# Adaptive average pooling: the sum over a tile in one VectorE instruction in place of a sum shared with GpSimd

## The chip, the cores and the metric

The kernel runs on one core of one Trainium2 chip. The metric is device time in microseconds (us), the median over several runs. One further execution was taken by the hardware profiler; durations below come from that one execution.

## The reference

The input `x` is float32, 32 x 256 x 4096. Each row of 4096 is cut into 256 windows of 16 neighbours, and each window is replaced by its mean:

```python
for i in range(output_size):                       # 256
    start = int(i * length / output_size)          # 16 * i
    end = int((i + 1) * length / output_size)
    result[:, :, i] = np.mean(x[:, :, start:end], axis=-1)
```

134.2 MB are read and 8.4 MB written. There is one addition per element read, and one multiplication per window.

## The kernel before

The 32 x 256 = 8192 rows are spread over 128 partitions. A tile is `xin`, 128 partitions by 16384 numbers (4 rows of 4096 each), or 1024 windows ("cells") of 16 in each partition, 8.39 MB. There are 16 tiles, in one Python loop over `t` that is written out in full. The pool `inpool` has two buffers for `xin`, so tile t+2 goes into the buffer of tile t.

Each turn of the loop issues, in this order:

- L74: the load of the tile, on SyncE's queue. It waits until its buffer's last reader is done.
- in the last turn only (t = 15), behind the load, the store `o_many` of the results of tiles 0 to 13 (`res_many`, 7.34 MB), by the helper at L61. It waits for ScalarE's scaling of tile 13.
- L77: GpSimd folds the upper half of the cells: in cells 512 to 1023, it adds the last 8 numbers of each window to the first 8, in place.
- L82: VectorE sums windows of 16 in the lower half of the cells (8192 numbers per partition).
- L85: VectorE sums the folded windows of 8 in the upper half (4096 numbers per partition). It waits for L77.
- L88: ScalarE multiplies the tile's 1024 sums by 1/16, in place in `res`.

After the loop the store `o_few` sends the results of tiles 14 and 15 (`res_few`, 1.05 MB), again by L61. All loads and stores are issued by SyncE in program order. The order of the rest follows from each engine's program order and from the semaphores that the tile framework puts in. The last reader of a tile is L85, and so L85 is what lets SyncE issue the load two tiles on.

Of the kernel before, what the change touches and what calls it, by code (L numbers as in the profile page):

```python
# [1 line left out]

# [4 lines left out]


@with_exitstack
def kernel(  # L10
    ctx: ExitStack,
    tc: tile.TileContext,
    x: bass.AP,
    output_size: int,
    out: bass.AP,
):

    nc = tc.nc
    F32 = mybir.dt.float32
    X = mybir.AxisListType.X

    batch, channels, length = x.shape
    ob, oc, olen = out.shape
    assert ob == batch and oc == channels and olen == output_size
    assert length % output_size == 0
    window = length // output_size  # L30
    hw = window // 2
    inv_w = 1.0 / float(window)

    P = nc.NUM_PARTITIONS
    R = 4
    tail = 2
    rows = batch * channels
    assert rows % (P * R) == 0
    ntiles = rows // (P * R)
    head = ntiles - tail  # L40
    many = head * R
    few = tail * R
    cells = R * output_size
    m = cells // 2
    cols = R * length

    xr = x.rearrange("b c l -> (b c) l")
    orow = out.rearrange("b c o -> (b c) o")
    x_many = xr[0 : P * many, :].rearrange("(p r) l -> p (r l)", p=P, r=many)
    o_many = orow[0 : P * many, :].rearrange("(p r) o -> p (r o)", p=P, r=many)  # L50
    x_few = xr[P * many :, :].rearrange("(p r) l -> p (r l)", p=P, r=few)
    o_few = orow[P * many :, :].rearrange("(p r) o -> p (r o)", p=P, r=few)

    res_many = nc.alloc_sbuf_tensor("res_many", [P, head * cells], F32, align_bytes=256)
    res_few = nc.alloc_sbuf_tensor("res_few", [P, tail * cells], F32, align_bytes=256)
    inpool = ctx.enter_context(tc.tile_pool(name="inpool", bufs=2))

    stored = nc.alloc_semaphore("stored")

    def store(out, in_):  # L60
        ins = nc.sync.dma_start(out=out, in_=in_)  # L61
        tc.no_tile_sem_insts.add(ins.ins.name)
        ins.then_inc(stored, 16)

    for t in range(ntiles):
        k = t - head
        xin = inpool.tile([P, cells, window], F32, name="xin")
        if k < 0:
            res, base = res_many, t * cells
            src = x_many[:, t * cols : (t + 1) * cols]  # L70
        else:
            res, base = res_few, k * cells
            src = x_few[:, k * cols : (k + 1) * cols]
        nc.sync.dma_start(out=xin.rearrange("p o w -> p (o w)"), in_=src)  # L74
        if t == ntiles - 1:
            store(o_many, res_many[:, :])
        nc.gpsimd.tensor_add(  # L77
            out=xin[:, m:cells, 0:hw],
            in0=xin[:, m:cells, 0:hw],
            in1=xin[:, m:cells, hw:window],  # L80
        )
        nc.vector.reduce_sum(  # L82
            out=res[:, base : base + m], in_=xin[:, 0:m, :], axis=X
        )
        nc.vector.reduce_sum(  # L85
            out=res[:, base + m : base + cells], in_=xin[:, m:cells, 0:hw], axis=X
        )
        nc.scalar.mul(  # L88
            out=res[:, base : base + cells],
            in_=res[:, base : base + cells],  # L90
            mul=inv_w,
        )
    store(o_few, res_few[:, :])

    ctx.pop_all().close()
    tc.close()
    tc.compile()  # L97
    nc.sync.wait_ge(stored, 32)
    nc.sync.sem_clear(stored)


# [1 line left out]
_INS = ['x', 'output_size']  # L103
_OUTS = [((32, 256, 256), 'float32')]

_NUMBERS = {'output_size': 256}


# [26 lines left out]
```

## Time and profile before

| | |
|---|---|
| median of 3 runs | 333.56 us (333.36 to 333.82) |
| time of the profiled execution | 333.14 us |
| its span in the profile | 331.8 us |
| moved by DMA | 142.61 MB, a mean of 430 GB/s |
| DMA engines' time in packets | 99.4% of 16 engines' span |
| VectorE busy | 209.7 us, 32 instructions |
| GpSimd busy | 139.7 us, 20 instructions, 16 of them the fold |
| ScalarE busy | 18.2 us |

The span is the stretch that the profile covers; the profiled execution took 1.3 us more than its span, and 0.4 us less than the median. Engine names in the profile: DVE is VectorE, POOL is GpSimd, ACT is ScalarE, SP is SyncE, and SPq is SyncE's sequencer as it issues DMAs. L82 is line 82 of the kernel. A group's line gives the tile written and the tile read with their shapes, the number of instructions, their busy time in us and the mean of one in ns, and then the engine's idle time just before them with what ended it.

### The profile page before, as it was taken

How to read it: one execution, taken by the hardware profiler on the slowest of the kernel's cores; microseconds unless marked ns; L12 is line 12 of the kernel's file. 1: busy time of each engine (PE TensorE's matmuls, PEld its weight loads, DVE VectorE, ACT ScalarE, POOL GpSimd, SP SyncE). 2: the span in 40 equal slices, each digit the busy share in tenths (PEclk: the TensorE clock that was granted, in tenths of full speed). 3: DMA queues.
4: the chain of work that ended last, by engine and by line, in shares of the span. 5: the costliest groups of instructions: out<-in, count | busy, mean ns of one | idle time of the engine just before them, and what ended most of it. 6: DMA issues, size and time to landing. Idle time of an engine off the chain costs nothing.

```text
span 331.8 us, 159 instructions
## 1 busy us (share of the span) xinstructions
DVE 209.7 (63%) x32; ACT 18.2 (5%) x17; POOL 139.7 (42%) x20
## 2 busy tenths in 40 slices
DVE  0029396692939669392966939295693929569392
ACT  1000101001010100001010000101000010100001
POOL 0027090642709164270906437090643709063370
DMA  9898989989898998989899898989899898989998
GB/s 379 379 506 379 506 379 411 474 379 506 379 506 379 427 458 379 506 379 506 379 458 427 379 506 379 506 379 498 387 403 482 379 506 379 506 379 442 411 442 348
DMA packets 2592, 142.61 MB, mean 430 GB/s; under 512 B 288, under 2 KB 288, under 8 KB 288
## 3 DMA queue, kind: packets, MB, share of 16 engines
q1 hardware_dynamic: 2592, 142.61, 99.4%
HBM read 134.22 MB, written 8.39 MB: 430 GB/s over the span
## 4 chain that ended last, share of the span: by engine, by line
DMA 66%; POOL 18%; DVE 11%; POOLq 3%; issue 0%; ACT 0%; SPq 0%
DMA xin<-in_x_dram 66%; POOL xin L77 18%; DVE res_many L85 9%; POOLq L97 3%; DVE res_few L85 1%; ACT res_few L88 0%; SPq L74 0%; POOLq L77 0%
## 5 line engine op out<-in xcount | busy, mean ns | idle before, releaser
L77 POOL TENSOR_TENSOR xin<-xin 128x4096 f32<-128x4096 f32 x16 | 139.5, 8717 | 181.4 <-DMA xin<-in_x_dram 181.4
L82 DVE TENSOR_REDUCE res_many<-xin 128x512 f32<-128x8192 f32 x14 | 121.6, 8686 | 101.3 <-DMA xin<-in_x_dram 101.3
L85 DVE TENSOR_REDUCE res_many<-xin 128x512 f32<-128x4096 f32 x14 | 61.9, 4420 | 2.3 <-POOL xin L77 2.1
L88 ACT ACTIVATE res_many<-res_many 128x1024 f32<-128x1024 f32 x14 | 14.8, 1056 | 271.3 <-DVE res_many L85 271.3
L82 DVE TENSOR_REDUCE res_few<-xin 128x512 f32<-128x8192 f32 x2 | 17.4, 8686 | 12.1 <-DMA xin<-in_x_dram 12.1
L85 DVE TENSOR_REDUCE res_few<-xin 128x512 f32<-128x4096 f32 x2 | 8.8, 4420 | 0.3 <-POOL xin L77 0.3
L88 ACT ACTIVATE res_few<-res_few 128x1024 f32<-128x1024 f32 x2 | 2.1, 1056 | 36.6 <-DVE res_few L85 36.6
L88 ACT ACT_TABLE_LOAD x1 | 1.3, 1283 | 0.7 <-PEq L116 0.7
L116 POOL MEMSET const-float32-0.0<- 128x1 f32 x1 | 0.1, 98 | 0.2 <-issue 0.2
L116 POOL MEMSET const-uint8-127<- 128x1 uint8 x1 | 0.1, 102 | 0.0
L116 POOL MEMSET const-bfloat16-1.0<- 128x1 bf16 x1 | 0.1, 101 | 0.0
L116 POOL MEMSET const-float32-1.0<- 128x1 f32 x1 | 0.1, 99 | 0.0
## 6 DMA issues: line engine op xcount, KB each, us to landing
out_dram<-res_many SPq DMA_DIRECT2D x1, 7168.0 KB, 41.2
out_dram<-res_few SPq DMA_DIRECT2D x1, 1024.0 KB, 4.9
xin<-in_x_dram SPq DMA_DIRECT2D x16, 25.4
```

Of the source, the lines that this page charges most:

```text
L77: nc.gpsimd.tensor_add(out=xin[:, m:cells, 0:hw], in0=xin[:, m:cells, 0:hw], in1=xin[:, m:cells, hw:window],)
L82: nc.vector.reduce_sum(out=res[:, base : base + m], in_=xin[:, 0:m, :], axis=X)
L85: nc.vector.reduce_sum(out=res[:, base + m : base + cells], in_=xin[:, m:cells, 0:hw], axis=X)
L88: nc.scalar.mul(out=res[:, base : base + cells], in_=res[:, base : base + cells], mul=inv_w,)
L97: tc.compile()
L116: nc = _bacc.Bacc("TRN2", target_bir_lowering=False, num_devices=1)
```

## The change

GpSimd's fold (L77) and the second sum (L85) are taken out. VectorE sums all 1024 windows of 16 in one instruction (16384 numbers per partition). The loads, the stores, the scaling, the two buffers and the order of the loop stay as they are.

```diff
-    hw = window // 2
...
-    m = cells // 2
...
         nc.sync.dma_start(out=xin.rearrange("p o w -> p (o w)"), in_=src)
         if t == ntiles - 1:
             store(o_many, res_many[:, :])
-        nc.gpsimd.tensor_add(
-            out=xin[:, m:cells, 0:hw],
-            in0=xin[:, m:cells, 0:hw],
-            in1=xin[:, m:cells, hw:window],
-        )
-        nc.vector.reduce_sum(
-            out=res[:, base : base + m], in_=xin[:, 0:m, :], axis=X
-        )
-        nc.vector.reduce_sum(
-            out=res[:, base + m : base + cells], in_=xin[:, m:cells, 0:hw], axis=X
-        )
+        nc.vector.reduce_sum(out=res[:, base : base + cells], in_=xin[:, :, :], axis=X)
         nc.scalar.mul(
             out=res[:, base : base + cells],
             in_=res[:, base : base + cells],
             mul=inv_w,
         )
```

## The prediction

> **What bounds the kernel now.** I read the page's queue and group parts first, to see which resource is full.
>
> ```profile
> q1 hardware_dynamic: 2592, 142.61, 99.4%
> L77 POOL TENSOR_TENSOR xin<-xin 128x4096 f32<-128x4096 f32 x16 | 139.5, 8717 | 181.4 <-DMA xin<-in_x_dram 181.4
> L82 DVE TENSOR_REDUCE res_many<-xin 128x512 f32<-128x8192 f32 x14 | 121.6, 8686 | 101.3 <-DMA xin<-in_x_dram 101.3
> L85 DVE TENSOR_REDUCE res_many<-xin 128x512 f32<-128x4096 f32 x14 | 61.9, 4420 | 2.3 <-POOL xin L77 2.1
> L88 ACT ACTIVATE res_many<-res_many 128x1024 f32<-128x1024 f32 x14 | 14.8, 1056 | 271.3 <-DVE res_many L85 271.3
> ```
>
> The DMA engines hold packets 99.4% of the span. VectorE sits idle before L82 because it waits for loads. So the transfers bound the kernel, and compute costs nothing as long as every transfer is issued before the one ahead of it has run out. How early they are issued stands in two other views. First SyncE's own waits:
>
> ```profile
> SPq L74 <- DVE res_many L85: 185.8, 14, 13.3
> ```
>
> Each of the 14 reloads is issued 13.3 us after the buffer's earlier tile has landed, when L85 is done. Tiles land every 19.33 us: the first L82 starts at 22.50 and the sixteenth at 312.47, and 289.97 / 15 = 19.33. So a reload has 19.33 - 13.3 = 6.0 us of lead over the landing of the load that is still running. Then the end, in the timeline (start, duration, instruction):
>
> ```profile
> 312.47 8.69 DVE L82 TENSOR_REDUCE res_few<-xin 128x512 f32<-128x8192 f32 x1 [6.10 <-DMA xin<-in_x_dram]
> 321.33 4.42 DVE L85 TENSOR_REDUCE res_few<-xin 128x512 f32<-128x4096 f32 x1 [0.17 <-POOL xin L77]
> 325.78 1.06 ACT L88 ACTIVATE res_few<-res_few 128x1024 f32<-128x1024 f32 x1 [18.32 <-DVE res_few L85]
> 326.86 0.34 SPq L61 DMA_DIRECT2D out_dram<-res_few  x1
> ```
>
> and the page's issues (size, us from issue to landing):
>
> ```profile
> out_dram<-res_many SPq DMA_DIRECT2D x1, 7168.0 KB, 41.2
> out_dram<-res_few SPq DMA_DIRECT2D x1, 1024.0 KB, 4.9
> ```
>
> The large store, issued at 288.18 (timeline), lands 41.2 us later, at 329.4: it queues behind the last load and then needs 312.47 to 329.4, 16.9 us. It hides the last sum, the scaling and the issue of the small store, whose 1 MB then follows straight on. That store lands at 326.86 + 4.90 = 331.76, the end of the span.
>
> **The new sum.** L82 and L85 differ by 4096 numbers and 8686 - 4420 = 4266 ns: 1.0415 ns a number, and 154 ns fixed in each. One instruction over 16384 numbers is then 16384 x 1.0415 + 154 = 17.22 us. L82 runs beside GpSimd's fold and L85 after it, and one straight line with a fixed part carries both, so I expect nothing from GpSimd's silence. A tile's sum now ends at 8.69 + 0.17 + 4.42 = 13.28 us after it starts; afterwards at 17.22, which is 3.94 us later. VectorE's load per tile, 17.22, stays under 19.33, so VectorE does not become the bound by its rate. GpSimd's 139.5 us and the 0.17 us waits lie inside the 13.28, and their removal brings nothing more.
>
> **The reloads (14).** SyncE issues a reload 0.03 us after the sum (the first L85 ends at 31.30 + 4.42 = 35.72, the issue is at 35.75), so now 17.25 us after the landing: the lead falls from 6.0 to 19.33 - 17.25 = 2.08 us. Does that cover the way from issue to first byte and from last byte to landing? The only load with nothing ahead of it is the first: issued at 0.74, landed at 22.50, so 21.76 us, of which 19.33 is the transfer and 2.43 the rest. By that price a buffer turns around in 17.25 + 21.76 = 39.01 us, against two transfers in 38.66: 0.35 us too long. The first issue instruction is itself slower than the others (426 ns against 328, the issue line's own view), and I take these 0.10 off: 0.25 us. Two buffers take turns, so a late reload delays the tile behind it no further: its own buffer is late by the same. So the loss comes once in two loads. From tile 1 to tile 15 there are seven turns: 7 x 0.25 = **1.75 us**. The bounds are 0 (the steady reload is quicker than the first by 0.35) and 7 x 0.35 = 2.45 at the first load's full price. No steady reload in this trace ever waits for its issue, so the value is the first load's row, the nearest there is.
>
> Where the 2.43 us lie is seen in windows at the start (a packet's time is counted in the window in which it starts, which is why the DMA share, the last column but one, can exceed 1):
>
> ```profile
> 0.70:1.60 0.90, 0.00 (x0) 0.86 (x1) 0.00 (x0) 1.00 0.00 0
> 1.60:2.80 1.20, 0.00 (x0) 0.42 (x1) 0.00 (x0) 1.00 2.52 874
> 21.40:22.40 1.00, 0.00 (x0) 0.00 (x0) 0.00 (x0) 1.00 2.43 1049
> ```
>
> First packets begin 0.9 to 2.1 us after the issue; the second load's first packets, which follow the first load's last ones, begin in 21.40 to 22.40, that is 0.1 to 1.1 us before tile 0's sum starts. So most of the 2.43 lies before the first byte, and this is the part that a reload needs its lead for. The Trainium skill, in "DMA: Bandwidth & Descriptors", section "Anatomy of one DMA", says of its (GpSimd-issued) DMAs that a fixed cost of about 2 us is dominated by completion, not by setup; by that the reload loss would be 0 and the sum 3.79 us, as in the first rival below; this trace's windows speak against it.
>
> **The end.** Counted from the last tile's start (312.47): sum 17.22, ScalarE 0.03 later for 1.06, issue 0.02 later, so the small store is issued at +18.33, where it was +14.39. The large store is over by then (+16.9), so nothing hides the small one any more. Unqueued, I price it like the first load without the 0.10: 2.33 us plus its 1 MB at the loads' rate, 19.33 / 8 = 2.42, together 4.75. It lands at +23.08 against +19.29 (331.76) before: **3.79 us**. Above: the 4.90 us that it took before, when it also stood in the queue: 18.33 + 4.90 - 19.29 = 3.94. Below: first byte after 0.9 us (the earliest of the windows), 2.42, and 0.4 for landing (its last packets begin in 331.20 to 331.40, by the windows, and it lands at 331.76): 18.33 + 3.72 - 19.29 = 2.76. I stay near the upper end, as the first load's row is a whole measured latency and the lower end is put together from earliest parts.
>
> Nothing else lies on the path: the other fifteen scalings wait for VectorE with 271.3 us to spare in total, and the large store, now released at about tile 13's start + 18.3, still queues behind load 15, which SyncE issued 1.1 us before it.
>
> **Sum.** 1.75 + 3.79 = 5.5 us. The profiled execution of 333.14 would become 338.7; against the median of the runs, 0.42 higher, 333.56 + 5.5 = **339.1 us**. A difference under 0.2% (0.7 us) would not be told from none here.
>
> **The rivals.**
>
> *The reloads stay hidden* (33%). A reload's descriptors are ready while the load ahead still runs, so only the time to the first packet counts, and the earliest packets of the first load begin 0.9 us after the issue. With those 0.9 us and 0.1 to 1.1 between last byte and landing, a lead of 2.08 us is enough. Then only the end pays: 333.56 + 3.79 = 337.4, down to 336.3 by the lower bound. Against it: the late packets of the same load begin only 2 us after the issue, and a tile has landed only when the last of them has.
>
> *Restarting a running queue costs more than the first start* (11%). While another load runs, a new one may reach its first byte later than in an idle machine. If that is 0.3 us more, 7 x 0.3 = 2.1 on top: 341.2; at 0.6, 343.3. Nothing in the trace shows it, because no steady load comes that late.
>
> *VectorE alone is quicker than beside GpSimd* (4%), the one on the other side. Both work on the same tile in L82 and L77; if sharing slows VectorE, the lone instruction would gain. It decides at a sum of about 13.3 us, 0.80 ns a number in place of 1.04: then reloads and the small store are issued no later than now, and the time stays 333.6, since the transfers fill 99.4%. A still quicker sum would bring nothing but the start of the span's last store, which is queued anyway. Against it stands L85, which has no fold beside it and the same rate. That the change does not reach the engine as written is no separate case: the built kernel has 16 sums with 128x1024 outputs, and no GpSimd work but four constants.
>
> **How the numbers follow.** The forecast has 52%, its own range is 337.4 to 340.0 (0 + 3.79 to 2.45 + 3.94). The range to give reaches down into the hidden case, whose lower tail ends at 336.3, and up to the restart case at 0.3 us: 336.5 to 341.3. It leaves out the last rival, the dearer half of the restart case and a few per cent of the lowest ends, some 15%. All but the last rival are slower by more than 0.7 us: slower 0.96, same 0.03, faster 0.01.
>
> **What would show each step.** The sum: one group with 128x1024 outputs at 17.2 us, and SyncE's wait for VectorE at 17.2 each. The reloads: issue to landing near 21.7 in place of 25.4, tiles landing 19.33 and 19.6 us apart by turns, the last tile's sum starting 1.75 us later than 312.47, and DMA near 98%. The end: the small store issued 18.3 us after the last tile's start and landing 4.75 us later. If the last tile starts at 312.5, the reloads were hidden; if sums take under 13.3 us, the rate was wrong; if tiles land more than 19.7 us apart on the mean, a restart is dearer than the first start.

## The result and the profile after

The changed kernel takes **353.71 us** (median of 6 runs, 351.98 to 355.19) against 333.48 us before (6 runs): a ratio of 1.0603, 95% interval 1.0589 to 1.0618, 20.2 us slower. The profiled execution took 353.8 us with a span of 352.5.

The page's queue part and the sum's group answer first:

```profile
q1 hardware_dynamic: 2592, 142.61, 96.0%
L75 DVE TENSOR_REDUCE res_many<-xin 128x1024 f32<-128x16384 f32 x14 | 241.1, 17220 | 64.5 <-DMA xin<-in_x_dram 64.5
```

The sum is what was worked out, 17220 ns, but the DMA engines now hold packets for only 96.0% of a span that is 20.7 us longer. SyncE's waits say when the reloads are issued:

```profile
SPq L72 <- DVE res_many L75: 241.1, 14, 17.2
```

That is 17.2 us after the landing, as predicted. Where the time goes is seen in the timeline: each tile's sum starts when the tile has landed (the first number), and then the end.

```profile
22.72 17.22 DVE L75 TENSOR_REDUCE res_many<-xin 128x1024 f32<-128x16384 f32 x1 [22.72 <-DMA xin<-in_x_dram]
...
42.01 17.22 DVE L75 TENSOR_REDUCE res_many<-xin 128x1024 f32<-128x16384 f32 x1 [2.07 <-DMA xin<-in_x_dram]
...
63.15 17.22 DVE L75 TENSOR_REDUCE res_many<-xin 128x1024 f32<-128x16384 f32 x1 [3.91 <-DMA xin<-in_x_dram]
...
83.29 17.22 DVE L75 TENSOR_REDUCE res_many<-xin 128x1024 f32<-128x16384 f32 x1 [2.93 <-DMA xin<-in_x_dram]
...
104.43 17.22 DVE L75 TENSOR_REDUCE res_many<-xin 128x1024 f32<-128x16384 f32 x1 [3.91 <-DMA xin<-in_x_dram]
...
330.31 17.22 DVE L75 TENSOR_REDUCE res_few<-xin 128x1024 f32<-128x16384 f32 x1 [5.21 <-DMA xin<-in_x_dram]
347.57 1.06 ACT L76 ACTIVATE res_few<-res_few 128x1024 f32<-128x1024 f32 x1 [21.38 <-DVE res_few L75]
348.65 0.34 SPq L59 DMA_DIRECT2D out_dram<-res_few  x1
```

The first two loads stand 19.29 us apart as before. Then the distances are 21.14, 20.14 and 21.14 us where a transfer takes 19.33. From the first to the sixteenth tile it is 330.31 - 22.72 = 307.59 us against 289.97 before: **17.6 us are lost in the loop**. From the last tile's start to the end of the span (352.5) it is 22.2 us against 19.4: **2.8 us are lost at the end**. The other 0.2 is the first load's. The issues (KB each, median us from issue to landing):

```profile
out_dram<-res_few SPq DMA_DIRECT2D x1, 1024.0 KB, 3.8
xin<-in_x_dram SPq DMA_DIRECT2D x16, 24.1
```

A reload takes 24.1 us from issue to landing, not the 21.7 that the first load and the prediction had. How the first reload, issued at 39.97, is taken up is seen in windows (the DMA share is the last column but one; a packet counts where it starts):

```profile
39.50:41.00 1.50, 0.44 (x1) 1.02 (x1) 0.00 (x0) 1.00 0.00 0
41.00:42.00 1.00, 0.00 (x0) 0.03 (x1) 0.00 (x0) 1.00 1.77 655
42.00:43.00 1.00, 0.99 (x1) 0.00 (x0) 0.00 (x0) 1.00 1.05 393
```

The load ahead landed at 42.01, yet in 42.00 to 43.00 first packets of the reload still begin, up to 3 us after its issue. The 16 DMA engines start unevenly, and the latest sets the landing. It is plainest in the sixth reload, issued at 142.01:

```profile
142.80:143.80 1.00, 0.00 (x0) 0.28 (x1) 0.00 (x0) 1.00 2.13 721
143.80:144.80 1.00, 0.70 (x1) 0.00 (x0) 0.00 (x0) 1.00 0.76 262
145.30:145.80 0.50, 0.50 (x1) 0.00 (x0) 0.00 (x0) 1.00 0.43 131
```

A load's packet has 65.5 KB, so the last column (GB/s) gives 11, 4 and 1 first packets. The sixteenth engine begins over 3.2 us after the issue, and the tile lands 24.2 us after it, at 166.25.

Not all of the longer span is idle time of the engines. Packets hold 99.4% of 331.8 us before and 96.0% of 352.5 after, 329.8 against 338.4. So 8.6 of the 20.7 us are packets that take longer, and 12.1 are gaps. In the windows above, the first reload's 16 first packets (655 and 393 GB/s, together 1.05 MB) take 1.77 + 1.05 = 2.8 us each in the mean, where a packet in full flow takes 19.33 / 8 = 2.42.

### The profile page after: what moved, and what is told of

It reads as the page before. It is cut to its first block, busy times and chain, and to the rows that moved or that the text cites. A ratio compares the mean times of both kernels' runs of the same rounds, so it can differ in the third digit from the quotient of the medians.

```text
span 352.5 us, 111 instructions
## 1 busy us (share of the span) xinstructions
DVE 275.5 (78%) x16; ACT 18.2 (5%) x17; POOL 0.2 (0%) x4
## 4 chain that ended last, share of the span: by engine, by line
DMA 59%; DVE 39%; ACT 0%; issue 0%; SPq 0%
DMA xin<-in_x_dram 59%; DVE res_many L75 34%; DVE res_few L75 5%; ACT res_few L76 0%; SPq L72 0%
## 5 line engine op out<-in xcount | busy, mean ns | idle before, releaser
L75 DVE TENSOR_REDUCE res_many<-xin 128x1024 f32<-128x16384 f32 x14 | 241.1, 17220 | 64.5 <-DMA xin<-in_x_dram 64.5
L75 DVE TENSOR_REDUCE res_few<-xin 128x1024 f32<-128x16384 f32 x2 | 34.4, 17220 | 7.6 <-DMA xin<-in_x_dram 7.6
## 6 DMA issues: line engine op xcount, KB each, us to landing
xin<-in_x_dram SPq DMA_DIRECT2D x16, 24.1
```

What stands on the lines that cost most here:

```text
L75: nc.vector.reduce_sum(out=res[:, base : base + cells], in_=xin[:, :, :], axis=X)
```

## The experiments

Two theories stood at the start. By the prediction's own, a reload has a fixed price of 2.43 us beside its transfer (its sum took 0.10 off), and loses what its lead lacks of that. By its rival, a reload costs more while another load still runs; theory A and theory B in the expectations are forms of this one, and say each time which. Where no number of runs is given, a kernel ran once; the changed kernel's own runs spread over 3.2 us, so smaller differences between such kernels say nothing. A reload's lead is taken from the timeline: the start of the sum on the tile ahead, less the issue.

**The end alone.** Only the last tile is summed in one instruction.

```diff
+        if t == ntiles - 1:
+            nc.vector.reduce_sum(out=res[:, base : base + cells], in_=xin[:, :, :], axis=X)
+        else:
             ...   # fold and two sums as before
```

> Tiles 0 to 14 as before the change, only the last tile summed in one instruction. So the reloads keep their lead of 6.0 us and only the end is changed. Theory (loop and end are two separate costs): the last tile's sum starts at 312.5 us as before, and the end costs what it cost in the changed kernel, 22.1 us from the last sum's start to the end against 19.3, so +2.8 us: 336.3 us. The prediction's own price for the end: +3.8, 337.3 us. Rival (the end is dear only because the loads before it are uneven): under +2 us.

Measured: 336.14 us against 333.49 (ratio 1.0077, interval 1.0060 to 1.0094), +2.65. The timeline of its end and its issue line:

```profile
312.69 17.22 DVE L78 TENSOR_REDUCE res_few<-xin 128x1024 f32<-128x16384 f32 x1 [6.03 <-DMA xin<-in_x_dram]
329.94 1.06 ACT L91 ACTIVATE res_few<-res_few 128x1024 f32<-128x1024 f32 x1 [22.19 <-DVE res_few L78]
331.03 0.34 SPq L61 DMA_DIRECT2D out_dram<-res_few  x1
```

```profile
out_dram<-res_few SPq DMA_DIRECT2D x1, 1024.0 KB, 3.8
```

The last tile starts as before, and the small store is issued 18.3 us later, both as predicted. But the store lands 3.8 us after its issue, not 4.75: an unqueued store of 1 MB costs 1.4 us beside its 2.42 us of transfer (at the loads' rate), not the load's 2.33. The end is a separate cost, and the loop's loss is not needed for it.

**The loop alone, and every other tile alone.** The same `if` with `t < ntiles - 1`, and with `t % 2 == 0`.

> The change in all tiles but the last, whose sum is shared with GpSimd as before. If loop and end are separate, the changed kernel's 353.7 us less the 2.65 us that the change of the last tile alone cost: 351.1 us. If the uneven loads before it also lengthen the end: under 350 us.

Measured: 350.03 us (two runs, 349.17 and 350.88; ratio 1.0498, interval 1.0388 to 1.0609), 16.6 us over before. With the end's 2.65 that is 19.3 of the 20.2 us, and the difference is inside the spread of the runs. Within that spread, loop and end add up.

> Even tiles summed in one instruction as after the change, odd tiles with GpSimd's fold and two sums as before. So each of the seven turns has one reload with a lead of about 2.08 us and one with 6 us or more, behind which the DMA engines can even out; the end is as before the change. Fixed price of 2.43 us: 0.35 us a turn, 336 us. A late reload costs about 1.8 us by itself (as the changed kernel's first one did), and the rest of its loss came from engines left uneven for the next: 7 x 1.8 = 12.6 us, 346 us. All of the loss of the changed kernel comes from the even tiles' reloads alone: 17.6 us, 351 us.

Measured: 347.6 us. Here are its timeline's tile starts around the first two and the sixth of the seven late reloads (a line with 8192 numbers is an odd tile, with 16384 an even one):

```profile
41.95 8.69 DVE L85 TENSOR_REDUCE res_many<-xin 128x512 f32<-128x8192 f32 x1 [2.08 <-DMA xin<-in_x_dram]
...
63.64 17.22 DVE L78 TENSOR_REDUCE res_many<-xin 128x1024 f32<-128x16384 f32 x1 [8.47 <-DMA xin<-in_x_dram]
...
83.18 8.69 DVE L85 TENSOR_REDUCE res_many<-xin 128x512 f32<-128x8192 f32 x1 [2.32 <-DMA xin<-in_x_dram]
...
105.10 17.22 DVE L78 TENSOR_REDUCE res_many<-xin 128x1024 f32<-128x16384 f32 x1 [8.63 <-DMA xin<-in_x_dram]
...
246.63 8.69 DVE L85 TENSOR_REDUCE res_many<-xin 128x512 f32<-128x8192 f32 x1 [2.69 <-DMA xin<-in_x_dram]
...
265.95 17.22 DVE L78 TENSOR_REDUCE res_many<-xin 128x1024 f32<-128x16384 f32 x1 [6.04 <-DMA xin<-in_x_dram]
```

The first two even tiles here stand 21.7 and 21.9 us behind the tile ahead (41.95 to 63.64, 83.18 to 105.10), the odd tile between them, whose reload came much earlier, 19.5; the last even tile shown stands only 19.3 behind. The seven late reloads cost 2.4, 2.6, 2.8, 0.5, 2.3, 0.0 and 1.6 us over a transfer: 12.2 us, a mean of 1.74, where the prediction had 0.25 each. Six of them had leads of 2.0 to 2.3 us (the tile's start less the issue, 17.25 us after the start two tiles back); the sixth, which cost nothing, had 246.63 - 226.72 - 17.25 = 2.7. The loop loses 326.95 - 22.65 - 289.97 = 14.3 us here, of which 1.5 lie in the last load. Taking the odd tiles' early reloads away as well brings 3.3 us more. So the late reloads by themselves bring most of the loss, and at almost the same lead it differs much from turn to turn (0.5 at 2.15 us, 2.8 at 2.04).

The expectation counted on the engines evening out behind an early reload. Windows on the last packets ahead of the first late reload (issued at 39.90) and ahead of the second (80.88) show that they do not:

```profile
38.50:39.50 1.00, 1.00 (x1) 0.00 (x0) 0.00 (x0) 1.00 2.42 1049
78.00:79.00 1.00, 1.00 (x1) 0.00 (x0) 0.00 (x0) 1.00 0.91 393
79.00:80.00 1.00, 1.00 (x1) 0.00 (x0) 0.00 (x0) 1.00 1.21 524
80.00:81.00 1.00, 0.85 (x1) 0.11 (x1) 0.00 (x0) 1.00 0.32 131
```

The load that queued behind the first one starts its last 16 packets (1049 GB/s for 1 us) within 1 us. The odd tile's load, issued 8 us ahead, starts them spread over three windows of 1 us (6, 8 and 2 packets). So the first late reload, with even engines ahead, shows 2.4 us of its own; what uneven engines add to the later ones, or take off, this run does not separate.

**Idle starts.** `bufs=1`: nothing else is in flight when a load is issued.

> The changed kernel with one buffer for the tiles in place of two: every load is issued when nothing else is in flight. Theory A (a restart is dear only while another load still runs on the same queue): every load takes what the first one takes, 21.8 us from issue to landing; 15 turns of 17.25 + 21.8 us, the last sum starts at about 608 us and the span is about 630 us. Theory B (every load after the first pays about 24 us, whatever is in flight): 15 turns of 41.3 us, a span of about 664 us.

Measured: 633.0 us, span 631.7. Its issue line, and windows around its second load, issued at 39.79:

```profile
xin<-in_x_dram SPq DMA_DIRECT2D x16, 21.8
```

```profile
38.80:40.80 2.00, 0.97 (x1) 1.00 (x1) 0.00 (x0) 1.00 0.51 164
40.80:41.80 1.00, 0.00 (x0) 0.06 (x1) 0.00 (x0) 1.00 2.13 721
41.80:42.80 1.00, 0.00 (x0) 0.00 (x0) 0.00 (x0) 1.00 0.00 0
```

The loads take what the first one took, a median of 21.8; their issue instructions, but for the first, take 328 ns. This load's first packets begin 1 to 2 us after the issue, and none later than 41.80. They take 2.00 x 0.51 + 2.13 = 3.15 us each in the mean, so longer first packets are a part of the idle price too. So the first load's price, on which the prediction stood, is right for an idle machine. It was no cold start, and it is not what a reload pays beside a running load.

**The lead, longer.** The sum over a part of each window, `xin[:, :, 0:12]`, `0:14`, `0:15`; the other numbers are left out.

> The changed kernel with the sum over 12 of each 16 numbers (the other four are left out): 12288 numbers, 12.95 us, so a lead of 6.35 us for each reload, as in the kernel before, but with one VectorE instruction and no GpSimd. If only the lead matters: 333.5 us, last sum from 312.5 us. If the one long instruction over the whole tile, or GpSimd's absence, harms the transfers in another way: more than 335 us, with tiles further apart than 19.33 us.

Measured: 333.39 us. One long instruction without GpSimd harms nothing.

> The changed kernel with the sum over 14 of each 16 numbers (the other two are left out): 14336 numbers, 15.1 us, so a lead of 4.2 us for each reload. Fixed price of 2.43 us for a load (the prediction's): no loss in the loop, the last sum starts at 312.5 us, and the end is 0 to 1 us later than before: 333.5 to 334.5 us. Theory A with a need of more than 4.2 us: a loss in the loop of several us, 335 to 345 us, and first packets longer than 2.42 us.

Measured: 333.85 us. The waits of SyncE and the queue:

```profile
SPq L72 <- DVE res_many L75: 211.2, 14, 15.1
```

```profile
q1 hardware_dynamic: 2592, 142.61, 99.2%
```

At a lead of 4.2 us the loop loses nothing. The small store, issued 16.2 us after the last tile's start, is still nearly hidden.

> The changed kernel with the sum over 15 of each 16 numbers (the last is left out): 15360 numbers, 16.15 us, a lead of 3.15 us. Fixed price (2.43 us for a load issued late, whatever else runs): no loss in the loop, only the end, about 335.3 us. Theory A (a reload that reaches a DMA engine during its last packet is taken up like a fresh start after that packet, so the need is 2.43 us plus up to a packet of 2.42): part of the engines are late, a loss of 2 to 15 us in the loop, 337 to 350 us.

Measured: 347.27 us. The first two reloads at this lead of 3.15 us cost nothing and 0.6, later ones up to 1.6, the last 3.2; the loop loses 324.86 - 22.53 - 289.97 = 12.4 us. So 3.15 is already too short, and the fixed price falls here. It is not the lead alone, either: many of these reloads had leads of 3.4 to 4.7, and the one that lost 1.6 had 4.1, where 4.2 cost nothing in the kernel above.

**The lead, shorter.** A ScalarE instruction reads and writes a part of the tile after the sum, so that the buffer comes free later while VectorE does the same as in the changed kernel.

```diff
+        if t < ntiles - 2:
+            nc.scalar.mul(out=xin[:, 0:64, :], in_=xin[:, 0:64, :], mul=inv_w)
```

The cut shows 64 cells, 1024 numbers; the two others have 16 and 256 cells.

> The changed kernel with a ScalarE instruction over 256 numbers of the tile (a multiplication in place, of which nothing is used) after the sum, about 0.42 us: lead 1.63 us, between the changed kernel's 2.08 and the 1.0 that gave 348.5 us. Fixed price of 2.43 us: 0.8 us a turn, 5.6 us, with the end 341.8 us. If reloads are still met by engines that are in their last packet: 346 to 355 us.

Measured: 358.17 us, above both ranges, and slower than the kernels with more lead (2.08) and with less (1.0). The first reload, at a lead of 1.6, lost 2.0 us.

> The changed kernel with one more ScalarE instruction per tile that touches 1024 numbers of the tile after the sum (a multiplication in place, of which nothing is used) ahead of the scaling, so that the buffer is free 1.1 us later: the lead of a reload falls from 2.08 to 1.0 us. Fixed price of 2.43 us: 1.4 us lost in each of seven turns, 10 us, with the end 346 us. Fixed price of 4.5 us (what the changed kernel's reloads took over their transfer): 3.5 us a turn, 25 us, 361 us. Theory A (the engines start afresh after their last packet, whether the reload came 2 or 1 us before): hardly more than the changed kernel, 353 to 357 us.

Measured: 348.46 us, **5 us faster than the changed kernel, though every buffer comes free 1.1 us later**. Its tile starts and its issue line:

```profile
41.84 17.22 DVE L75 TENSOR_REDUCE res_many<-xin 128x1024 f32<-128x16384 f32 x1 [2.06 <-DMA xin<-in_x_dram]
...
62.93 17.22 DVE L75 TENSOR_REDUCE res_many<-xin 128x1024 f32<-128x16384 f32 x1 [3.87 <-DMA xin<-in_x_dram]
...
82.24 17.22 DVE L75 TENSOR_REDUCE res_many<-xin 128x1024 f32<-128x16384 f32 x1 [2.09 <-DMA xin<-in_x_dram]
...
103.28 17.22 DVE L75 TENSOR_REDUCE res_many<-xin 128x1024 f32<-128x16384 f32 x1 [3.82 <-DMA xin<-in_x_dram]
```

```profile
xin<-in_x_dram SPq DMA_DIRECT2D x16, 21.9
```

The reloads take 21.9 us, the idle price, and even tiles lose 1.5 to 1.8 us each. By 2.43 - 1.0 it should be 1.43. The odd tiles between, whose reload then has a lead of 2.5 to 2.75 us, lose nothing, but for the last, which loses 1.2. Windows at the first reload, issued at 40.90:

```profile
40.80:41.80 1.00, 0.00 (x0) 1.00 (x2) 0.00 (x0) 1.00 0.01 0
41.80:42.80 1.00, 0.96 (x1) 0.02 (x1) 0.00 (x0) 1.00 3.06 1049
```

The load ahead landed at 41.84, and all 16 first packets (1049 GB/s for 1 us) begin at about that time or after it, within 1.9 us of the issue: the reload meets engines that have finished, as in an idle machine. Theory A, as written for this run (hardly any difference from the changed kernel), falls.

> As the kernel with one more ScalarE instruction, but over 4096 numbers: the buffer is free about 3.5 us later, the lead is about -1.5 us, and each reload is issued when nothing else is in flight. Theory A: the price of an idle start, 21.8 us from issue to landing, 4.0 us lost in each of seven turns: 28 us, with the end 364 us. A price of 24.1 us from issue to landing for every reload: 6.3 us a turn, 44 us, 380 us.

Measured: 366.01 us, and 21.8 us from issue to landing: the idle price, as expected.

The seven kernels side by side; the lead is the one worked out for the first late reload, the loop's loss is the way from the first tile's start to the last one's, less 289.97, and the fixed price is seven turns of 2.43 less the lead:

| lead of a late reload, us | loop's loss, us | by a fixed price of 2.43, us |
|---|---|---|
| 6.35 (12 of 16 numbers) | 0.3 | 0 |
| 4.2 (14 of 16) | 0.0 | 0 |
| 3.15 (15 of 16) | 12.4 | 0 |
| 2.08 (the change) | 17.6 | 2.5 |
| 1.63 (ScalarE, 256 numbers) | 22.1 | 5.6 |
| 1.0 (1024) | 12.4 | 10.0 |
| -1.6 (4096) | 29.7 | 28.2 |

In these totals the fixed price holds nearly at both ends, where the machine is idle when the reload's packets begin or where there is ample lead, and there is a hump between about 4 and 1 us.

The cleanest comparison is the first reload of each kernel, as the load ahead of it is the same in all. Measured leads of 3.13, 2.04, 1.59, 0.94 and -1.62 us lost 0, 1.8, 2.0, 1.8 and 4.1, where the fixed price gives 0, 0.4, 0.8, 1.5 and 4.1. The two kernels above that have a part of the change and the same first reload, at 2.04, lost 2.0 and 2.4. So beside a running load, at 1.6 to 2.0 us of lead, a reload paid 1.2 to 2.0 us more than by the idle price.

Later reloads depend on more than their lead, and a reload that loses time lengthens the lead of the next one. Of the changed kernel's 14 reloads, nine had leads of 2.0 to 3.1 us and lost 15.4 in sum, from nothing to 3.1 each; five had 3.9 to 4.95 and lost 2.3. In the kernels at 1.0 and -1.6, the odd reloads had 2.3 to 2.75 and, but for the last, lost 0 to 0.2, as the fixed price has it. The load ahead of these had met idle engines. What a load leaves of the engines' evenness may thus matter as well as the lead; no run varies it by itself.

**Smaller packets.** A tile takes rows that do not lie next to each other, so that a piece is 16 KB.

```diff
-    x_many = xr[0 : P * many, :].rearrange("(p r) l -> p (r l)", p=P, r=many)
+    x_many = xr[0 : P * many, :].rearrange("(p r s) l -> p r s l", p=P, r=R)
...
+            res, src = v_many[:, :, t, :], x_many[:, :, t, :]
```

> The changed kernel with other rows in a tile: four rows of a partition that do not lie next to each other, so that a load consists of pieces of 16 KB in place of 64 KB (packets of about 0.6 us in place of 2.4). Sums, bytes, lead (2.08 us) and the results are the same. Theory A (the time that an engine's last packet takes is part of the need): the loss in the loop shrinks to a third or less, 336 to 343 us. Theory B (only the time from issue to the engines counts, slower while another load runs): the same loss, 350 to 356 us. If small pieces are slow in themselves, tiles are further apart and the issue to landing of the first load is over 21.8 us.

Measured: 355.22 us, as the changed kernel, and 331.74 - 22.97 - 289.97 = 18.8 us lost in the loop. Theory A falls by this total: packets a quarter as large do not shrink the loss. The first reload alone lost less, 0.6 us at a lead of 2.17, where the changed kernel's lost 1.8 at 2.04; the later ones lost up to 3.2.

**Two queues.** Odd loads and the stores from ScalarE's queue; then only the even loads from tile 2 on.

> The changed kernel with the odd tiles' loads and the two stores issued by ScalarE (its own queue) and the even tiles' loads by SyncE; each reload is issued right after its sum as before, lead 2.08 us. So a reload goes to a queue that has been empty for a whole tile, while the DMA engines still work on the other queue. Theory A (what is slow is a reload that reaches a queue just as that queue runs out): the engines take it up in time, the loop loses 0 to 2 us, with the end's 2.65 us 336 to 338 us. Theory B (what is slow is a reload that reaches a busy DMA engine near its end, whatever the queue): 350 to 356 us.

Measured: 374.15 us, and not a test of the question. The first two loads, on two queues, ran side by side and landed at 41.80 and 41.97; from then on two sums ran back to back, and then two loads side by side.

> The changed kernel with the loads of tiles 2, 4, ... 14 issued by ScalarE right after the sum that frees the buffer, all other loads and the stores by SyncE. Tiles 0 and 1 start on one queue, one behind the other. Lead 2.08 us; each reload goes to a queue whose last load ended a whole tile ago, while the DMA engines end a load of the other queue. Theory A (slow is a reload that reaches a queue which is running out): engines take it up in time, even share themselves between both queues at the seam; the loop loses 0 to 3 us, 336 to 339 us. Theory B (slow is a reload that reaches a busy DMA engine near its end, whatever the queue): 350 to 356 us.

Measured: 356.76 us. The timeline shows that the pairs fell into the same step after the first seam (x2 is two sums back to back):

```profile
39.86 0.37 ACTq L73 DMA_DIRECT2D xin<-in_x_dram  x1
65.95 34.34 DVE L85 TENSOR_REDUCE res_many<-xin 128x1024 f32<-128x16384 f32 x2 [6.83 <-DMA xin<-in_x_dram]
83.20 0.33 ACTq L73 DMA_DIRECT2D xin<-in_x_dram  x1
107.42 34.34 DVE L85 TENSOR_REDUCE res_many<-xin 128x1024 f32<-128x16384 f32 x2 [7.12 <-DMA xin<-in_x_dram]
```

So the total tells nothing, but the first seam does, in windows. The reload was issued at 39.86 on a queue that had never been used, while the other queue's load ran out and landed at 41.90:

```profile
39.50:41.00 1.50, 0.33 (x1) 0.74 (x1) 0.00 (x0) 1.00 0.00 0
41.00:42.00 1.00, 0.10 (x1) 0.99 (x2) 0.00 (x0) 1.00 1.50 524
42.00:43.00 1.00, 1.00 (x1) 0.61 (x1) 0.00 (x0) 1.00 1.50 524
```

As in the changed kernel, first packets still begin in 42.00 to 43.00. ScalarE's queue is not slow in itself: its next reload, issued at 83.20 with no other load in flight, has its 16 first packets in one stretch of 1.3 us, 0.9 to 2.2 us after the issue:

```profile
84.10:85.40 1.30, 1.30 (x1) 0.54 (x1) 0.00 (x0) 1.00 2.43 807
```

On the one seam, then, the late take-up goes with the busy DMA engines, not with a queue that runs out: theory B. Whether the first use of a queue beside a running load adds to it is not separated.

**Half tiles, two buffers.** `R = 2`, `tail = 4`.

> The changed kernel with tiles of half the size (2 rows in a partition, 32 tiles) and two buffers: a sum takes 8.69 us, a transfer 9.67, the lead is 0.95 us. Price of an idle start (2.43 us), as in the kernel with a lead of 1.0: 1.48 us lost in each of fifteen turns, 22 us; the end is hidden behind the large store: 355.7 us. Price of 4.7 us as in the changed kernel's reloads: 3.75 us a turn, 390 us.

Measured: 380.15 us, between both prices. The lead did not stay at 0.95: the first late reload made the next one's lead 2.4 us and the third's 2.2, and those landed 13.3 and 15.0 us after their issue where the first load took 12.0.

**Half tiles, four buffers.** The same with `bufs=4`.

> The changed kernel with tiles of half the size and four buffers, so the same bytes of buffers: one VectorE sum of 8.69 us per half tile, no GpSimd, and a reload is issued with about 20 us of transfers still ahead of it. Theory (the loss comes from the short lead and from the last tile's long sum alone): both go away, 333.0 to 333.6 us, the same as the kernel before. If one sum over everything without GpSimd costs in another way: over 335 us.

Measured: 333.79 us (11 runs) against 333.35 (15 runs), ratio 1.0014, interval 1.0005 to 1.0023. Queue, and timeline of the end:

```profile
q1 hardware_dynamic: 4896, 142.61, 99.6%
```

```profile
313.01 8.69 DVE L75 TENSOR_REDUCE res_few<-xin 128x512 f32<-128x8192 f32 x1 [1.04 <-DMA xin<-in_x_dram]
321.73 0.63 ACT L76 ACTIVATE res_few<-res_few 128x512 f32<-128x512 f32 x1 [9.10 <-DVE res_few L75]
322.38 0.34 SPq L59 DMA_DIRECT2D out_dram<-res_few  x1
```

The loss is gone with one VectorE sum per tile and no GpSimd. The last sum is half as long, so the small store goes out while the large one runs. It does not beat the kernel before, as transfers already filled that one's time.

## Why the prediction was wrong

Its direction, and the two places at which it put the loss, were right; its size was not: 5.5 us were forecast and 20.2 measured.

- **The sum**: 17.22 us forecast and measured. GpSimd's silence changed nothing, as argued. The rival on the other side (VectorE quicker alone) falls.
- **The lead**: 2.08 us forecast; the first reload had 2.04.
- **The reloads**: this step failed. Its term of 1.75 us measured 17.6. The prediction priced a reload by the first load, 2.43 us over its transfer, because it was the only row with nothing ahead of it, and took 0.10 off. The idle-start kernel shows that price to be right for an idle machine (a median of 21.8 over all its loads). The 0.10 was a misreading: the 426 ns are the second load's issue instruction, the first load's takes 383, and the idle starts' 328 brought no quicker landing. That is worth 0.7 us over seven turns, and not the failure. But a reload with 2.08 us of lead is not issued into an idle machine. The first took 63.15 - 39.97 = 23.2 us and the median 24.1, 3.9 to 4.8 over the transfer, and a turn lost 2.5 us on average in place of 0.25. The engines took the first one up later than idle ones would, up to 3 us after the issue. "A late reload delays the tile behind it no further" was nearly right: with every other tile changed, the late reloads alone lose 12.2 us, and the loop's other loads 2.1. The upper bound of 2.45 us was no bound, since no row of the trace before had a late reload in it.
- **The rivals**: "restarting a running queue costs more", given 11%, is the one that came, with 2.3 us more a turn where it was priced at 0.3 to 0.6. The sign named for it, tiles more than 19.7 us apart on the mean, stands in the trace: 307.59 / 15 = 20.5. "The reloads stay hidden" came true at a lead of 4.2 us, not at 2.08. The Trainium skill says in "DMA: Bandwidth & Descriptors", section "Anatomy of one DMA", of DMAs issued by GpSimd, that completion dominates the fixed cost; by that these reloads would have been hidden at 2.08. The windows show up to 3 us before the first packet, and so speak against it for these loads from SyncE's queue.
- **The end**: 3.79 forecast, 2.8 in the profile and 2.65 alone. The mis-sized term is the unqueued store: 3.8 us in place of 4.75. The lower bound, 2.76, put together from earliest parts, was nearer than the load's row; that it fits so well is luck, as no run shows its parts one by one.

What stays open is why an engine that is ending one load takes up the next one later. The runs show when it happens and that neither the packet's size, by the total, nor, at one seam, the queue decides; they do not see inside the DMA engines. The Trainium skill, in "DMA: Bandwidth & Descriptors", section "Latency and other measured facts", gives an HBM access as 0.2 us on average and 2 us at high load. Whether that has a part in it, no run here separates. Nor do the runs say why the last load lost another 1.1 to 1.5 us in several of these kernels. It is the one with the large store behind it, and with one buffer the load ahead of that store took 23.0 us where the others took 21.8; but in the kernel before, the last load lost nothing.

## What to carry to other kernels

Transfers that fill the span hide compute only as long as each is issued well before the one ahead ends: read that lead from the DMA queue's own waits, and ask what a longer compute step leaves of it. Do not price an issue beside a running transfer by an idle first one; here the loop lost seven to ten times what that price said. More and smaller buffers of the same total size buy lead, and shorten what stands after the last load.

## What was not expected of the hardware

The loss is not monotonic in the lead. 4.2 us of lead cost nothing, 2.08 us cost 17.6 us, and 1.0 us cost 12.4: freeing the buffer 1.1 us later made the kernel 5 us faster, and its reloads took what they take in an idle machine. And nearly equal leads have different prices from turn to turn, 0.5 to 2.8 us at leads of 2.0 to 2.3 with every other tile changed. That would fit the changed kernel's runs spreading over 3.2 us where those of the kernel before spread over 0.5, but no run shows the link.
